# Moving TensorE operands by 64 bytes in a two-layer trunk: constants, some low parts, and seven 16-column products

## The chip, the cores and the metric

The kernel runs on one core of one Trainium2 chip. The metric is the device time of one execution in microseconds (us), the median of several. Below, TensorE is PE, VectorE is DVE, ScalarE is ACT, GpSimd is POOL and SyncE is SP.

## The reference

A decoder trunk of two layers over 512 tokens and 1024 channels, float32. Layer 0 mixes tokens by retention, layer 1 by an mLSTM, each with 4 heads of 256 query and key columns and 512 value columns; each layer ends in a convolutional feed-forward net (FFN) of 2816 inner columns. Cut to what matters:

```python
for i in range(2):
    mod = silu(c) @ ada_w[i] + ada_b[i]                  # 6 vectors of 1024
    h = rmsnorm(x, norm_tok_g[i]) * (1 + sc_t) + sh_t
    y = retention(h) if i == 0 else mlstm(h)             # heads: q, k, v, gate, group norm, out
    x = x + gt_t * y
    h = rmsnorm(x, norm_ffn_g[i]) * (1 + sc_f) + sh_f
    x = x + gt_f * (silu(a) * b) @ w_down                # a, b = split(conv(h @ w_up))
return rmsnorm(x, final_g)
```

## The kernel before, in words

**Precision.** Matrix products run in TensorE's fp32r form on operands that are split in a high and a low part. A product of two split matrices is three TensorE products: high by high, high by low, low by high. In names, `whi` and `wlo` are the parts of a weight tile, `hh` and `hl` of the normalized input `h`, `yh` and `yl` of a head's output, `ggh` and `ggl` of an FFN's gated columns, and so on. A weight tile has 128 partitions and 1024 columns of 4 bytes, in a buffer of 1088 columns; most tiles begin at column 0 of their buffer, some at column 16 (`OFF`, 64 bytes later).

**Folded products.** Most projections don't use the plain block product but one of seven products for eight (`seven`, in the order 1, 2, 6, 5, 7, 4, 3). Their weights are sums and differences of weight blocks, built by DVE from two loaded tiles (`wa`, `wb` or several `wv`, through `ws` and `wt`), at column 16 of their buffers; each product is 256 columns wide. A `PairStream` has the weight blocks as TensorE's stationary operand and the tokens moving (banks `p`), a `ValueStream` the tokens stationary and the weights moving (banks `pv`). `terms(n, k)` gives the token side. DVE evacuates a product's bank by adding a copy `fs` to it (`p<-p,fs`).

**Stages.** Start and first norm to about 88 us, the heads of layer 0, the output projection with the next norm's square sums mixed in (`boundary`, near 386 us), the FFN, then the same for layer 1. `heads` sets the sequence of a layer: `q(0)`, `q(1)`, ... each with attention steps and, after `g(1)`, the first output projection `o(0)`; `contract_items` runs an output projection of one head, `boundary` the last ones, in two halves of 256 tokens, with weights at column 16. `boundary` already opens with a product of 16 columns whose result nothing reads (`short_product`), and so do the folded FFN runs (`folded`). The square sums of a norm come from `SquareSum.root`, which multiplies by a constant matrix `ones_d` of 1/1024 (bank `pms`); `ones_v` (group norm, `pmu` and `pvar`) and `ones_1` (sums, `pden`, and products that keep TensorE busy while the first loads run, `pst<-warm`) are its two relations. Between the projections DVE also computes the modulation vectors, one load `ada` of 128x1025 at a time.

**Order.** No engine's order is written by hand. All calls are recorded by a class `Plan`, so each has the line L377 in the profile, and then a planner lists them by estimated costs, due times and the number of free buffers per kind, and issues them in that order. A queue issues in order: SP, which issues most loads, waits at a load whose buffer is not free, and so do those behind it. Numbers in names of the listings below count tiles; the last is the call's position in the program.

Of the kernel before, what the change touches and what calls it, by code (L numbers as in the profile page):

```python
# [10 lines left out]
F32 = mybir.dt.float32  # L11
F32R = mybir.dt.float32r
# [4 lines left out]
P = 128  # L17
T = 512
D = 1024
KT = D // P  # L20
# [16 lines left out]
WPAD = 64  # L37
OFF = 16
# [342 lines left out]
def trunk(ctx: ExitStack, tc: tile.TileContext, xT, cb, pos, vec, ident, decay, zmask, ada, w_s0, w_in0, w_v0,  # L381
          w_o0, w_in1, w_v1, w_f1, w_o1, w_up, w_dn, out):
    nc = tc.nc
    const = ctx.enter_context(tc.tile_pool(name="const", bufs=1))
# [10 lines left out]
    def uid(s):  # L395
        count[0] += 1
        return f"{s}_{count[0]}"

    def tile_of(pool, shape, dt, tag, name):
        return Buf(pool, shape, dt, tag, name, KINDS.get(tag, 0), tag == "ps")  # L400

    def slot(s, dt=F32, w=T):
        return tile_of(slots, [P, w], dt, "s", uid(s))

    def wide(s, dt=F32):
        return tile_of(wpool, [P, WCOLS + WPAD], dt, "w", uid(s))

    def bank(s):
        return tile_of(psum, [P, T], F32, "ps", uid(s))
# [4 lines left out]
    def fixed(pool, shape, dt, name):  # L414
        b = tile_of(pool, shape, dt, name, name)
        b.get()
        return b

    plan = Plan()
    V, A, G, PE, S = (plan.engine(*p) for p in (("DVE", nc.vector), ("ACT", nc.scalar), ("POOL", nc.gpsimd),  # L420
                                                ("PE", nc.tensor), ("SP", nc.sync)))
# [3 lines left out]
    V.memset(fixed(const, [P, 32], F32, "pad")[:], 0.0)  # L425
    ones = {}
    for name, v in (("d", 1.0 / D), ("v", 1.0 / DV), ("1", 1.0)):
        o = fixed(const, [P, P], F32R, f"ones_{name}")
        V.memset(o[:].bitcast(F32), v)
        ones[name] = o  # L430


# [56 lines left out]
        return lo  # L489

    class Chunk:
        def __init__(self, src, n, off, added=False):
            self.off, self.added = off, added
            self.raw = wide("raw")[:, off : off + n]
            S.dma_start(self.raw, src)

# [1 line left out]
            self.hi = high_part(self.raw, self.off)  # L498

        def low(self):  # L500
            self.lo = (low_part_added if self.added else low_part)(self.raw, self.hi, self.off)

        def lo_at(self, at, k):
            return at * P
# [115 lines left out]
    class Pair:  # L620
# [3 lines left out]
        def split(self, src, r=slice(None), eng=None):  # L624
            A.copy(self.hi[:, r], src)
            (eng or V).tensor_tensor(self.lo[:, r], src, self.hi[:, r].bitcast(F32), op=ALU.subtract)
# [6 lines left out]
    def mm3(o, ah, al, bh, bl, start, stop):  # L633
        PE.matmul(o, ah, bh, start=start, stop=False)
        PE.matmul(o, ah, bl, start=False, stop=False)
        PE.matmul(o, al, bh, start=False, stop=stop)

    def short_product(o, w, b):


        PE.matmul(o, w, b, start=True, stop=True, skip_group_check=True)
# [64 lines left out]
    class Use:  # L706


        def __init__(self, src, n, off=0, added=False):
            self.src, self.n, self.first, self.off, self.added = src, n, None, off, added  # L710

        def make(self):
            c = Chunk(self.src, self.n, self.off, self.added)
            c.high()
            c.low()
            return c
# [16 lines left out]
    def item(uses, fn, free=True):  # L733
        for u in uses:
            if u.first is None:
                u.first = len(items)
            u.last = len(items)
        items.append((uses, fn, free))
# [1 line left out]
    bars = []  # L740
    side = []

    def proj_item(src, h, then, added=False):
        def fn(w):
            ps = bank("pp")
            for k in range(KT):
                cs = slice(k * P, k * P + P)
                mm3(ps[:], w[0].hi[:, cs], w[0].lo[:, cs], h[k].hi[:], h[k].lo[:], k == 0, k == KT - 1)
            then(ps)
        item([Use(src, KT * P, added=added)], fn)  # L750

    ORDER = (1, 2, 6, 5, 7, 4, 3)

# [42 lines left out]
                PE.matmul(o, b[0][:, ts], lo[:, cs], start=False, stop=False, skip_group_check=True)  # L796
                PE.matmul(o, b[1][:, ts], hi[:, cs], start=False, stop=sp, skip_group_check=True)

    def seven(use, streams, done, between=lambda j: None):


        fs = []

        def mk(n):
            def fn(w):
                if n == ORDER[0]:
                    for s in streams:
                        s.open(w[0])
                        fs.append(slot("fs"))
                for s, f in zip(streams, fs):  # L810
                    o = {1: s.c21, 2: s.c11, 5: s.c12, 3: s.c12}.get(n, s.c21)
                    s.product(n, o, n in s.starts)
                    if n in (1, 6, 7):
                        A.copy(f[:, HB if n == 6 else HA], s.c21)
                    if n == 7:
                        V.tensor_tensor(s.c22, s.c12, f[:, HA], op=ALU.add)
                    elif n == 2:
                        V.tensor_tensor(s.c11, s.c11, f[:, HA], op=ALU.add)
                    elif n == 3:
                        V.tensor_tensor(s.c12, s.c12, f[:, HB], op=ALU.add)  # L820
                if n == 3:
                    done(*[s.banks for s in streams])
            return fn
        for j, n in enumerate(ORDER):
            item([use], mk(n), j in FREE_STEPS)
            between(j)

    def fold_pairs(srcs, terms, thens, between=lambda j: None):

        def each(then):  # L830
            def done(bs):
                for b in bs:
                    then(b)
            return done
        for n, (src, then) in enumerate(zip(srcs, thens)):
            seven(FoldUse(src, n), [PairStream(terms, then)], each(then), lambda j: between(7 * n + j))

    def fold_values(src, terms, v, split, between=lambda j: None):

        def done(a, b):  # L840
            for ps in (a[0], b[0], a[1], b[1]):
                split(v, ps)
        seven(ValueFoldUse(src, 0), [ValueStream(terms, t) for t in range(2)], done, between)

    def folded(folds, h, terms, pairs, downs):

# [192 lines left out]
        return [piece(i) for i in range(KT // per)]  # L1039

    def contract_items(ps, between=lambda i: None):
        for i, (u, run) in enumerate(ps):
            item([u], lambda w, run=run: run(w[0], 0, T))
            between(i)
# [251 lines left out]
    def heads(st, q, v, s, g, a, mid, end, o, norm, at_last):  # L1296
# [13 lines left out]
        g(1)  # L1310
        A_(1)
        contract_items(o(0))
        mid_(1)
        q(2)
# [172 lines left out]
    def half_pair(st, name, finish):  # L1487

        got = []

        def then(ps):
            got.append(ps)
            if len(got) == 2:
                st[name] = finish(*got)
        return then

    h0 = []
    R = [dict(v=[], g=[], z=[]) for _ in range(H)]
# [10 lines left out]
    def ret_gate(i):  # L1509
        def then(ps):  # L1510
            g = slot("g")
            A.activation(g[:], ps[:], AF.Silu)
            R[i]["g"].append(g)
        return then
# [21 lines left out]
    def ret_start():  # L1536
# [4 lines left out]
        pss, ps = [bank("pst") for _ in range(5)], bank("pms")  # L1541
        pcs = [bank("pc") for _ in range(2)]
        pss += pcs
        one = ones["1"][:1, :].bitcast(F32)
        h0.extend(Pair("h") for _ in range(KT))
        wh, wl, raw, mod, sq, xrs = {}, {}, {}, {}, {}, {}

# [137 lines left out]
    sums0 = Sums(h0, {}, 0, 0)  # L1685

    def sums_early():
        sums0.make()
        sums0.turn()

    def pair_srcs(w, at):
        return [(w[at], w[at + 1]), (w[at + 2], w[at + 3])]

    def ret_q(i, between=nothing):
        thens = [half_pair(R[i], name, rope) for name in ("q", "k")]
        if i:
            fold_pairs(pair_srcs(w_in0, i * 8), sums0.terms, thens, between)
            return
        for n, then in enumerate(thens):
            for j in range(2):  # L1700
                proj_item(w_in0[i * 8 + 2 * n + j], h0, then)
        item([], lambda w: sums_early())

    def ret_g(i):
        fold_pairs(pair_srcs(w_in0, i * 8 + 4), sums0.terms, [ret_gate(i)] * 2)

    def ret_v(i, between=nothing):
        fold_values(w_v0[i - 1], sums0.terms, R[i]["v"], center_split, between)

    def load_x():  # L1710
        for m in range(KT):
# [14 lines left out]
    M = [dict(v=[], o=[], z=[], q=[], k=[]) for _ in range(H)]  # L1726
# [72 lines left out]
    def ml_gate(i):  # L1799
        def then(ps):  # L1800
            o = slot("o")
            A.activation(o[:], ps[:], AF.Sigmoid)
            M[i]["o"].append(o)
        return then
# [30 lines left out]

    def ml_q(i, between=nothing):
        thens = [lambda ps, name=name, n=iter((0, 1)): conv_then(i, name, next(n))(ps) for name in ("q", "k")]
        fold_pairs(pair_srcs(w_in1, 1 + i * 8), start1.sums.terms, thens, between)

    def ml_g(i):  # L1840
        fold_pairs(pair_srcs(w_in1, 5 + i * 8), start1.sums.terms, [ml_gate(i)] * 2)

    def ml_o(i):
        return pieces(lambda j: w_o1[i, j], 4, gate_col(1, 0), lambda k: M[i]["y"][k], i in O_ADDED)

    def ml_v(i, between=nothing):
        fold_values(w_f1[i - 1], start1.sums.terms, M[i]["v"], plain_split, between)

    start1 = Start([w_in1[j] for j in (0, 5, 6, 7)], h1, 1, 0, [gates, ml_gate(0), ml_gate(0), ml_gate(0)], True)
    ffn0.items(start1)  # L1850
# [152 lines left out]
```

## Time and profile before

| | before |
|---|---|
| median of 3 runs | 1513.67 us (1513.44 to 1513.98) |
| the profiled execution | 1513.25 us, of which the span is 1511.3 us |
| mean granted TensorE clock | 0.994 |
| busy share PE / PEld / DVE / ACT / POOL | 98% / 91% / 84% / 71% / 19% |
| HBM read | 195.23 MB, 131 GB/s over the span |
| the longest wait of PE | 5.5 us, for DVE, before 291.87 us |

All times of the profile count from the span's start. In a timeline a row has the start, the busy time of one or several instructions of a form, the engine, the line, the operation, what it writes from what it reads, and its shape; the idle time before it stands in brackets, with what ended it. A matmul's busy time overlaps with that of its successor, so a start-to-start distance says more of a stream of matmuls than their durations. In the windows a row has its length, then for each engine asked for its busy time and count, then the granted clock, the DMA share and GB/s.

### The profile page before, as it was taken

Reading aid. Unit: us, or ns where it says so; the run is one execution under the profiler, and the core shown is the slowest. Engines: PE = TensorE matmul, PEld = TensorE weight load, DVE = VectorE, ACT = ScalarE, POOL = GpSimd, SP = SyncE. Lnnn points to the kernel's source line nnn. Section 1 sums busy time; section 2 is a strip of 40 time slices with the busy share of each in tenths; the row PEclk is TensorE's granted clock in tenths of the full one; section 3 lists DMA queues with packets and bytes.
Section 4 is the critical chain, followed back from the end, with each engine's and each line's share of the span. In section 5 each row is a group of like instructions: output and inputs, shape, how many; then the busy total and the mean of one; then the engine's idle time right before and its main releaser. Section 6 shows DMA issues by size and latency. Waiting matters only on the chain.

```text
span 1511.3 us, 27097 instructions
## 1 busy us (share of the span) xinstructions
PE 1477.9 (98%) x10405; PEld 1375.5 (91%) x10405; DVE 1262.9 (84%) x2123; ACT 1069.0 (71%) x1593; POOL 281.6 (19%) x311
## 2 busy tenths in 40 slices
PE   9999999899999999999999999999999999999997
PEld 6889999798998989899998988999989899999997
DVE  6998989676887888888798999999877877877786
ACT  4558858777577666666578986899976867677662
POOL 0234222232111111111001222223131111111100
PEclk9999999999999999999999999999999999999999
DMA  9467999896487999999368887989875868787841
GB/s 375 158 161 204 282 272 275 207 236 148 103 224 202 244 265 255 271 260 253 115 168 223 206 234 202 262 216 248 223 179 136 213 171 196 173 207 182 204 127 56
DMA packets 92979, 314.98 MB, mean 208 GB/s; under 512 B 12193, under 2 KB 14625, under 8 KB 92850
## 3 DMA queue, kind: packets, MB, share of 16 engines
q0 software_dynamic: 31824, 115.88, 41.4%
q1 hardware_dynamic: 61026, 197.38, 36.7%
q8 instruction: 81, 1.33, 0.3%
q14 instruction: 48, 0.39, 0.1%
HBM read 195.23 MB, written 2.12 MB: 131 GB/s over the span
## 4 chain that ended last, share of the span: by engine, by line
PE 85%; DVE 6%; DMA 6%; ACT 2%; issue 1%; POOL 0%; SPq 0%; DVEq 0%; ACTq 0%; POOLq 0%
PE p L377 31%; PE po L377 25%; PE pv L377 9%; PE pp L377 6%; PE pf L377 4%; PE pav L377 4%; PE pst L377 3%; PE psc L377 2%; DMA wb<-w_up 1%; DMA ada<-ada 1%; PE pc L377 1%; ACT whi L377 1%; DVE ws L377 1%; DVE wlo L377 1%; DVE ada L377 1%
## 5 line engine op out<-in xcount | busy, mean ns | idle before, releaser
L377 PE MATMUL p<-hh,whi 128*128 128x256 f32 (+1 forms) x962 | 267.8, 279 | 5.8 <-DVE p L377 5.5
L377 PE MATMUL p<-hl,whi 128*128 128x256 f32 x960 | 266.8, 278 | 0.7 <-DVE hl L377 0.5
L377 PE MATMUL p<-hh,wlo 128*128 128x256 f32 x960 | 265.3, 278 | 1.5 <-DMA wlo<-wa 1.5
L377 ACT ACTIVATE wlo<-whi 128x1024 fp32r<-128x1024 f32 x221 | 233.2, 1059 | 45.5 <-PE po L377 22.0
L377 PEld LDWEIGHTS p<-hh,whi 128*128 128x128 f32 x962 | 181.5, 189 | 7.7 <-DVE p L377 6.0
L377 PEld LDWEIGHTS p<-hl,whi 128*128 128x128 f32 x960 | 181.3, 189 | 1.5 <-DVE hl L377 1.1
L377 PEld LDWEIGHTS p<-hh,wlo 128*128 128x128 f32 x960 | 180.3, 189 | 2.0 <-DMA wlo<-wa 1.9
L377 PE MATMUL p<-t24h,whi 128*128 128x256 f32 x720 | 161.3, 281 | 6.9 <-DVE p L377 4.2
L377 DVE SCALAR_TENSOR_TENSOR x<-po,mod,x 128x512 f32<-128x512 f32 (+1 forms) x184 | 113.6, 629 | 52.5 <-PE po L377 51.7
L377 PE MATMUL po<-ggh,wlo 128*128 128x512 f32 (+1 forms) x448 | 152.6, 343 | 0.8 <-DVE wlo L377 0.8
L377 PE MATMUL po<-ggl,whi 128*128 128x512 f32 (+1 forms) x448 | 153.1, 343 | 0.0
L377 PE MATMUL po<-ggh,whi 128*128 128x512 f32 (+1 forms) x448 | 152.6, 343 | 0.0
L377 ACT CAST whi<-raw 128x1024 fp32r<-128x1024 f32 (+1 forms) x121 | 121.8, 1019 | 26.0 <-PE po L377 7.8
L377 PE MATMUL p<-t24l,whi 128*128 128x256 f32 x480 | 133.6, 278 | 0.0
L377 PEld LDWEIGHTS p<-t24h,whi 128*128 128x128 f32 x720 | 123.0, 189 | 10.8 <-DVE p L377 5.9
L377 DVE SCALAR_TENSOR_TENSOR ada<-ada,c_ext 128x1025 f32<-128x1025 f32 x96 | 122.0, 1275 | 10.4 <-DMA ada<-ada 10.4
L377 POOL DMA_DIRECT2D wlo<-wa x60 | 53.0, 883 | 414.7 <-ACT wlo L377 320.1
L377 PE MATMUL po<-yh,whi 128*128 128x256 f32 (+1 forms) x354 | 116.0, 329 | 0.0
L377 PE MATMUL po<-yl,whi 128*128 128x256 f32 (+1 forms) x352 | 115.7, 329 | 0.0
L377 PE MATMUL po<-yh,wlo 128*128 128x256 f32 (+1 forms) x352 | 115.7, 329 | 0.0
L377 ACT CAST whi<-ws 128x1024 fp32r<-128x1024 f32 x84 | 88.0, 1050 | 30.9 <-DVE ws L377 22.3
L377 DVE TENSOR_TENSOR wlo<-raw,whi 128x768 fp32r<-128x768 f32 (+2 forms) x113 | 101.8, 915 | 7.7 <-ACT whi L377 3.6
(285 smaller groups left out, 4459.8 us busy)
## 6 DMA issues: line engine op xcount, KB each, us to landing
ada<-ada SPq DMA_DIRECT2D x96, 512.5 KB, 6.9
wlo<-ws POOLq DMA_DIRECT2D x71, 512.0 KB, 7.1
wlo<-wa POOLq DMA_DIRECT2D x60, 512.0 KB, 6.7
wlo<-wt POOLq DMA_DIRECT2D x44, 512.0 KB, 7.7
wlo<-raw POOLq DMA_DIRECT2D x40, 512.0 KB, 8.4
wa<-w_up SPq DMA_DIRECT2D x34, 512.0 KB, 5.8
wb<-w_up SPq DMA_DIRECT2D x34, 512.0 KB, 6.8
raw<-w_o SPq DMA_DIRECT2D x32, 512.0 KB, 7.2
```

Source lines behind the costliest of these rows:

```text
L377: getattr(c.obj, c.name)(*[real(v) for v in c.a], **{key: real(v) for key, v in c.k.items()})
```

## The change

Three things change. The constant matrices `ones_d`, `ones_v` and `ones_1` become 192 columns wide and are used from column 16 on, so their data begins 64 bytes later than before. `Chunk`, `Use` and `proj_item` get an argument `lo_off`: the low part of the last tile of each `contract_items` call, and that of the last key tile of layer 0's first head, begin at column 16 instead of 0. And `seven` gets an argument `lead`: seven of the folded calls open with a product of 16 columns, with `ones_1` as weights, into a part of a bank that nothing reads before it is written again. These are layer 0's `v` of head 1, `g` of head 2 and `q` of head 3, and layer 1's `q` of heads 1 and 3, `v` of head 1 and `g` of head 2. The constants' pool grows by 768 bytes a partition, so every other tile keeps its place modulo 128 bytes. The arithmetic is the same.

```diff
-        o = fixed(const, [P, P], F32R, f"ones_{name}")
-        V.memset(o[:].bitcast(F32), v)
+        o = fixed(const, [P, P + WPAD], F32R, f"ones_{name}")[:, OFF : OFF + P]
+        V.memset(o.bitcast(F32), v)
...
     class Chunk:
-        def __init__(self, src, n, off, added=False):
-            self.off, self.added = off, added
+        def __init__(self, src, n, off, added=False, lo_off=0):
+            self.off, self.added, self.lo_off = off, added, max(off, lo_off)
...
-            self.lo = (low_part_added if self.added else low_part)(self.raw, self.hi, self.off)
+            self.lo = (low_part_added if self.added else low_part)(self.raw, self.hi, self.lo_off)
...
-    def seven(use, streams, done, between=lambda j: None):
+    def seven(use, streams, done, between=lambda j: None, lead=False):
...
+                    if lead:
+                        short_product(streams[0].c22[:, :16], ones["1"], streams[0].terms(1, 0)[0][:, :16])
...
     def contract_items(ps, between=lambda i: None):
+        ps[-1][0].lo_off = OFF
...
-                proj_item(w_in0[i * 8 + 2 * n + j], h0, then)
+                proj_item(w_in0[i * 8 + 2 * n + j], h0, then, lo_off=OFF * n * j)
...
-            fold_pairs(pair_srcs(w_in0, i * 8), sums0.terms, thens, between)
+            fold_pairs(pair_srcs(w_in0, i * 8), sums0.terms, thens, between, i == 3)
...
-        fold_pairs(pair_srcs(w_in0, i * 8 + 4), sums0.terms, [ret_gate(i)] * 2)
+        fold_pairs(pair_srcs(w_in0, i * 8 + 4), sums0.terms, [ret_gate(i)] * 2, lead=i == 2)
...
-        fold_values(w_v0[i - 1], sums0.terms, R[i]["v"], center_split, between)
+        fold_values(w_v0[i - 1], sums0.terms, R[i]["v"], center_split, between, i == 1)
...
-        fold_pairs(pair_srcs(w_in1, 1 + i * 8), start1.sums.terms, thens, between)
+        fold_pairs(pair_srcs(w_in1, 1 + i * 8), start1.sums.terms, thens, between, i in (1, 3))
...
```

TensorE, layer 0, where the projection `q` of head 3 begins its second bank pair (`p2_589` is a half of it, `pav` the attention of head 2). Before:

```order
1621 L377 MATMUL pav_567_3102<-sh_522_3030,vh_509_2985 128x256
1622 L377 MATMUL pav_567_3102<-sl_523_3052,vh_509_2985 128x256
1623 L377 MATMUL pav_567_3102<-sh_522_3030,vl_510_3063 128x256
1624 L377 MATMUL p2_589_3124<-hh_24_237,whi_579_2853 128x256
1625 L377 MATMUL p2_589_3124<-hl_25_265,whi_579_2853 128x256
```

Of the changed kernel:

```order
1624 L377 MATMUL pav_567_3080<-sl_523_3092,vh_509_2987 128x256
1625 L377 MATMUL pav_567_3080<-sh_522_3032,vl_510_3090 128x256
1626 L377 MATMUL p2_589_3131<-hh_24_237,ones_1_81 128x16
1627 L377 MATMUL p2_589_3131<-hh_24_237,whi_579_2852 128x256
1628 L377 MATMUL p2_589_3131<-hl_25_265,whi_579_2852 128x256
```

The 16-column product stands directly ahead of the folded run, as it does in the six other places. The planner also lists three stretches of the heads otherwise than before, about 126 to 340, 830 to 895 and 1068 to 1100 us; the FFNs and the norms keep their order.

DVE, layer 0, before PE's longest wait. `ada_540` and `ada_539` are loads of the modulation, each step frees its buffer; `ws`, `wt` and `wlo` build folded weights; `wa_600` and `wb_601` are loaded tiles. Before:

```order
356 L377 SCALAR_TENSOR_TENSOR vl_506_3040<-vt_503_2822,vm_504_2823,vh_505_2979 128x512
357 L377 TENSOR_TENSOR sl_523_3052<-sp_521_2994,sh_522_3030 128x256
...
366 L377 TENSOR_TENSOR wt_605_3112<-wa_600_2826,ws_604_3087 128x512
367 L377 SCALAR_TENSOR_TENSOR ada_539_2814,mod_0_86<-ada_539_2814,c_ext_82 128x1025
368 L377 SCALAR_TENSOR_TENSOR ada_540_2981,mod_0_86<-ada_540_2981,c_ext_82 128x1025
369 L377 TENSOR_TENSOR p1_588_3142<-p1_588_3142,fs_590_3154 128x256
```

Of the changed kernel:

```order
356 L377 TENSOR_TENSOR wt_582_3041<-wa_577_2756,ws_581_2995 128x512
357 L377 TENSOR_TENSOR p1_536_2768<-p1_536_2768,fs_538_2772 128x256
358 L377 SCALAR_TENSOR_TENSOR ada_540_2983,mod_0_86<-ada_540_2983,c_ext_82 128x1025
359 L377 SCALAR_TENSOR_TENSOR vl_506_3077<-vt_503_2783,vm_504_2784,vh_505_2981 128x512
...
368 L377 TENSOR_TENSOR wt_605_3135<-wa_600_2830,ws_604_3101 128x512
369 L377 SCALAR_TENSOR_TENSOR ada_539_2801,mod_0_86<-ada_539_2801,c_ext_82 128x1025
370 L377 TENSOR_TENSOR p1_588_3152<-p1_588_3152,fs_590_3157 128x256
```

The step of `ada_540` moved from row 368 to row 358, ahead of ten rows that build weights and attention operands.

SP's queue at the same place (`tab` is a table of decays). Before:

```order
102 L377 DMA tab_511_2785<-decay 128x512
103 L377 DMA ada_539_2814<-ada 128x1025
104 L377 DMA wa_600_2826<-w_in0 128x1024
105 L377 DMA wb_601_2891<-w_in0 128x1024
106 L377 DMA ada_540_2981<-ada 128x1025
107 L377 DMA wv_624_3080<-w_v0 128x1024
108 L377 DMA ada_557_3149<-ada 128x1025
109 L377 DMA wv_622_3159<-w_v0 128x1024
```

Of the changed kernel:

```order
102 L377 DMA ada_539_2801<-ada 128x1025
103 L377 DMA tab_511_2809<-decay 128x512
104 L377 DMA wa_600_2830<-w_in0 128x1024
105 L377 DMA wb_601_2920<-w_in0 128x1024
106 L377 DMA ada_540_2983<-ada 128x1025
107 L377 DMA wv_624_3063<-w_v0 128x1024
108 L377 DMA ada_557_3082<-ada 128x1025
109 L377 DMA wv_622_3169<-w_v0 128x1024
```

Here only `tab` and `ada_539` have changed places. `ada_557` takes the buffer of `ada_539` in the order before and that of `ada_540` in the changed one, and `wv_622` stands behind it in both.

More of the change, by code (lines that the diff above doesn't have):

```diff
@@ L706, in trunk, with __init__ @@
     class Use:
-        def __init__(self, src, n, off=0, added=False):
-            self.src, self.n, self.first, self.off, self.added = src, n, None, off, added
+        def __init__(self, src, n, off=0, added=False, lo_off=0):
+            self.src, self.n, self.first, self.off, self.added, self.lo_off = src, n, None, off, added, lo_off
         def make(self):
-            c = Chunk(self.src, self.n, self.off, self.added)
+            c = Chunk(self.src, self.n, self.off, self.added, self.lo_off)
             c.high()
@@ L741, in trunk, with proj_item @@
     side = []
-    def proj_item(src, h, then, added=False):
+    def proj_item(src, h, then, added=False, lo_off=0):
         def fn(w):
@@ L749, in fn @@
             then(ps)
-        item([Use(src, KT * P, added=added)], fn)
+        item([Use(src, KT * P, added=added, lo_off=lo_off)], fn)
     ORDER = (1, 2, 6, 5, 7, 4, 3)
@@ L826, in seven, with fold_pairs @@
             between(j)
-    def fold_pairs(srcs, terms, thens, between=lambda j: None):
+    def fold_pairs(srcs, terms, thens, between=lambda j: None, lead=False):
         def each(then):
@@ L835, in fold_pairs, with fold_values @@
         for n, (src, then) in enumerate(zip(srcs, thens)):
-            seven(FoldUse(src, n), [PairStream(terms, then)], each(then), lambda j: between(7 * n + j))
-    def fold_values(src, terms, v, split, between=lambda j: None):
+            seven(FoldUse(src, n), [PairStream(terms, then)], each(then), lambda j: between(7 * n + j), lead and not n)
+    def fold_values(src, terms, v, split, between=lambda j: None, lead=False):
         def done(a, b):
@@ L842, in done @@
                 split(v, ps)
-        seven(ValueFoldUse(src, 0), [ValueStream(terms, t) for t in range(2)], done, between)
+        seven(ValueFoldUse(src, 0), [ValueStream(terms, t) for t in range(2)], done, between, lead)
     def folded(folds, h, terms, pairs, downs):
@@ L1543, in ret_start @@
         pss += pcs
-        one = ones["1"][:1, :].bitcast(F32)
+        one = ones["1"][:1].bitcast(F32)
         h0.extend(Pair("h") for _ in range(KT))
@@ L1837, in ml_q @@
         thens = [lambda ps, name=name, n=iter((0, 1)): conv_then(i, name, next(n))(ps) for name in ("q", "k")]
-        fold_pairs(pair_srcs(w_in1, 1 + i * 8), start1.sums.terms, thens, between)
+        fold_pairs(pair_srcs(w_in1, 1 + i * 8), start1.sums.terms, thens, between, i in (1, 3))
     def ml_g(i):
-        fold_pairs(pair_srcs(w_in1, 5 + i * 8), start1.sums.terms, [ml_gate(i)] * 2)
+        fold_pairs(pair_srcs(w_in1, 5 + i * 8), start1.sums.terms, [ml_gate(i)] * 2, lead=i == 2)
     def ml_o(i):
@@ L1846, in ml_v @@
     def ml_v(i, between=nothing):
-        fold_values(w_f1[i - 1], start1.sums.terms, M[i]["v"], plain_split, between)
+        fold_values(w_f1[i - 1], start1.sums.terms, M[i]["v"], plain_split, between, i == 1)
     start1 = Start([w_in1[j] for j in (0, 5, 6, 7)], h1, 1, 0, [gates, ml_gate(0), ml_gate(0), ml_gate(0)], True)
```

## The prediction, before the run

> **What bounds the kernel now.** I read the page's busy shares first, then the chain, then the list of waits.
>
> ```profile
> PE 1477.9 (98%) x10405; PEld 1375.5 (91%) x10405; DVE 1262.9 (84%) x2123; ACT 1069.0 (71%) x1593; POOL 281.6 (19%) x311
> PE 85%; DVE 6%; DMA 6%; ACT 2%; issue 1%; POOL 0%; SPq 0%; DVEq 0%; ACTq 0%; POOLq 0%
> PE p L377 <- DVE p L377: 9.7, 6, 5.5
> PE pv L377 <- DVE wlo L377: 0.8, 1, 0.8
> ```
>
> TensorE (PE) is busy 98% of the span and owns 85% of the last chain. There are two ways to a shorter time: the same products closer together, or shorter waits. The whole profiled execution took 1513.25 us, 1.95 more than its span of 1511.3, and lies 0.42 under the median of 1513.67. I sum against 1513.25 and add 0.42 at the end. 0.2% is 3.03 us, about what a measurement of this kernel can tell from no change.
>
> How close together are the products? The timeline of PE around the first normalization's square sums:
>
> ```profile
> 405.04 0.28 PE L377 MATMUL po<-yh,whi 128*128 128x256 f32 x1
> ...
> 405.72 0.28 PE L377 MATMUL pms<-ssh,ones_d 128*128 128x256 f32 x1
> ...
> 406.19 0.28 PE L377 MATMUL po<-yh,wlo 128*128 128x256 f32 x1
> ```
>
> From 405.04 to 405.72 six steps from start to start take 0.68 us, 113 ns each. The row at 405.72 is the first of a pair with `ones_d` as weights (tile `pms`, the squares' mean). From it to 406.19 four steps take 0.47 us, 118 ns each, in the same loop with the same shapes. The windows show that each pace lasts:
>
> ```profile
> 387.00:405.70 18.70, 18.70 (x167) 1.00 0.34 105
> 405.70:442.90 37.20, 37.20 (x318) 1.00 0.72 170
> 751.30:767.30 16.00, 15.97 (x134) 1.00 0.67 180
> 1146.20:1183.40 37.20, 37.20 (x318) 1.00 0.71 170
> 1487.00:1499.70 12.70, 12.70 (x110) 1.00 0.00 1
> ```
>
> A window counts the two products that are still running at its start, so it holds two starts fewer than its count: 18.70/165 = 113.3 ns before the pair, 37.20/316 = 117.7 after it, 12.70/108 = 117.6 at the end. The granted clock is 1.00 in all five. I call them the fast and the slow pace; one slow product costs 4.4 ns. What separates the pair is where its operands lie in their partitions. By the tile sizes in the code, the boundary's weights begin 64 bytes past a multiple of 128 and the moving tiles at a multiple; in the `pms` pair both begin at a multiple. That an even pair sets the slow pace, and that it then stays until something else resets it, is my reading of these rows. Two more fit it. A run that follows 512-column products with both operands even is slow; a run that follows one with odd weights (the low part of an FFN's last output tile) is fast:
>
> ```profile
> 198.55 0.28 PE L377 MATMUL p<-hh,whi 128*128 128x256 f32 x1
> ...
> 199.14 0.28 PE L377 MATMUL p<-hh,wlo 128*128 128x256 f32 x1
> ...
> 483.47 0.39 PE L377 MATMUL po<-ggl,whi 128*128 128x512 f32 x1
> 483.69 0.40 PE L377 MATMUL po<-ggh,wlo 128*128 128x512 f32 x1
> 483.93 0.28 PE L377 MATMUL p<-t3h,whi 128*128 128x256 f32 x1
> ...
> 484.39 0.28 PE L377 MATMUL p<-t3l,whi 128*128 128x256 f32 x1
> ```
>
> Five steps from 198.55 take 0.59 us, 118 ns each; four steps from 483.93 take 0.46 us, 115 ns each, the first of them still slow.
>
> **The change part by part. Constants.** With `ones_d` odd, the `pms` products get the boundary's own arrangement (odd weights, even moving), so nothing sets the slow pace at 405.72. Gain: 316 x 4.4 ns = 1.39 us at the first boundary, 1.39 at the third, 108 x 4.4 = 0.48 at the last. At the second (751 to 767) it is 132 x 4.4 = 0.58, but PE meets the wait of 0.8 us for DVE's `wlo` soon after, so I count 0.3. Sum 3.55. All of it is PE time on the chain, with no other engine late: in these windows PE is busy to the last hundredth. Bounds: 0, if the pair sets the pace for another reason than its address, and 3.84.
>
> **Low parts of the output tiles.** Each of six `contract_items` calls now has 8 products of 512 columns with odd weights. The row at 483.69 shows one: 0.24 us to the next start, where the one before takes 0.22. I take 16 ns each, 48 x 16 = 0.77 us; bounds 5 and 25 ns (0.24 and 1.2 us). The two calls of `o(0)` lie in the heads ahead of waits, so 32 x 16 ns = 0.51 counts. The 16 key products of the first head (0.26 us by the same price) lie ahead of DVE's waits and count nothing.
>
> **Leads.** Seven 16-column products, priced at the one that opens a boundary:
>
> ```profile
> 386.55 0.40 PE L377 MATMUL po<-yh,whi 128*128 128x16 f32 x2
> ...
> 387.02 0.28 PE L377 MATMUL po<-yh,whi 128*128 128x256 f32 x1
> ```
>
> From 386.55 to 387.02 stand one short product and three long ones (the first is counted in its row, x2): 0.47 - 3 x 0.113 = 0.13 us for the short one, 0.9 us for seven. Each may buy the fast pace for its call: 168 products x 4.4 ns = 0.74 us at most, 5.2 for seven, less what is fast already. But the heads are not bound by PE alone:
>
> ```profile
> 836.00:1083.00 247.00, 242.16 (x1851) 231.59 (x1850) 232.72 (x364) 211.60 (x322) 64.27 (x72) 1.00 0.89 230
> 200.00:260.00 60.00, 59.92 (x493) 58.75 (x492) 54.85 (x85) 44.77 (x71) 17.22 (x20) 1.00 1.03 277
> 260.00:270.00 10.00, 10.00 (x75) 9.64 (x74) 9.79 (x20) 8.73 (x12) 1.89 (x4) 1.00 0.60 171
> 290.00:300.00 10.00, 7.41 (x41) 7.12 (x42) 6.62 (x13) 4.39 (x6) 2.19 (x2) 0.66 0.79 182
> ```
>
> In the second layer's heads (836 to 1083) DVE, the third busy figure, works 232.72 of 247 us; in the first's (200 to 260) the DMA share is 1.03. A PE that comes sooner waits sooner. I count 0 for gains less leads, bounds -2.5 and +0.9. The other uses of the constants (the warm-up products at the start, `pmu`, `pvar`, `pden`) I put at 0.2 us together, an estimate by the same 16 ns for about a dozen that nothing covers. Without the order, then: -3.55 + 0.51 + 0.2 = **-2.8 us**.
>
> **The order.** The leads cost the planner TensorE time, and three stretches come out in another order (about 126 to 340, 830 to 895 and 1068 to 1100 us); the feed-forward nets keep theirs. The place where that can weigh is PE's longest wait:
>
> ```profile
> 291.87 0.58 PE L377 MATMUL p<-hh,whi 128*128 128x256 f32 x1 [5.47 <-DVE p L377]
> 258.55 0.33 SPq L377 DMA_DIRECT2D ada<-ada  x1
> 264.23 0.63 DVE L377 TENSOR_TENSOR sl<-sp,sh 128x256 fp32r<-128x256 f32 x2
> 270.38 1.23 DVE L377 SCALAR_TENSOR_TENSOR ada<-ada,c_ext 128x1025 f32<-128x1025 f32 x1
> 271.64 0.33 SPq L377 DMA_DIRECT2D ada<-ada  x1
> 272.07 1.63 SPq L377 DMA_DIRECT2D wv<-w_v  x2
> 287.51 2.82 DVE L377 SCALAR_TENSOR_TENSOR ada<-ada,c_ext 128x1025 f32<-128x1025 f32 x1 [3.55 <-DMA ada<-ada]
> 291.39 0.42 DVE L377 TENSOR_TENSOR p<-p,fs 128x256 f32<-128x256 f32 x1
> ```
>
> Read backwards: PE at 291.87 waits for the evacuation of a bank at 291.39, which stands on DVE behind the `ada` step at 287.51, which waited 3.55 us for its load; that load is behind two others that SP could issue only at 271.64, since an `ada` load stood in front until DVE's `ada` step of 270.38 freed its buffer. Meanwhile the DMA share fell to 0.60 (260 to 270). In the changed order DVE does `ada_540`'s step ten rows sooner, before the `sl` steps that began at 264.23, and the blocked load takes its buffer: free at about 264.8 + 1.2 = 266.0 (an estimate; two `wt` steps and an evacuation come before it) instead of 271.6, so that load goes into the idle stretch. The two `wv` loads behind it still need a buffer that DVE's `wt` reads about 271: only one load of 512 KB is out of their way, about 2 us at 277 GB/s. So the wait shrinks by about **2 us**. Bounds: the wait goes wholly, or grows by 4.
>
> A wait that shrinks below some length saves more:
>
> ```profile
> 295.24 0.41 PE L377 MATMUL p<-t3h,wlo 128*128 128x256 f32 x1
> 295.45 0.41 PE L377 MATMUL p<-t3h,whi 128*128 128x256 f32 x1
> ```
>
> After it the products start 0.21 us apart, at the granted clock of 0.66 that the window 290 to 300 shows, until about 296.7: (296.7 - 291.9)/0.21 = 23 products, each 0.1 us dearer, 2.2 us. The Trainium skill, page "TensorE: Matmul & The Clock Gate", Part 1, says the clock drops to half after an idle window of about 3.4 us; by it a wait cut to 3.4 us would save these 2.2 too. The row agrees for 5.47 us; no wait of 3 to 5 us is shown here. I count nothing for it.
>
> Forecast: 1513.25 - 2.8 - 2.0 = 1508.4, and 0.42 for the median: about **1508.8 us**.
>
> **The rivals.** (a) Only the boundaries gain, and the heads give back what the order saves: -2.8, so 1510.9, at the edge of what can be told. For it speaks DVE's 94% in the second layer's heads; against it the unused DMA stretch.
>
> (b) The long wait goes wholly, and with it the half clock: -2.8 - 5.5 - 2.2 + 0.9 (the leads then count) = -9.6, so 1504.1. Against it: the `wv` loads' buffer.
>
> (c) Slower: `ada_540`'s step now stands sooner in DVE's queue than its load lands. That load was issued at 258.55; DVE reaches the step about 264.8. If it lands at 268.3, DVE stands 3.5 us with `ws`, `wt` and `wlo` of two folded tiles behind it, and the `wv` loads that need their buffers go out as much later. The wait at 286 then grows by 3.5, and a second wait of like size, with a half clock of its own, opens where the delayed `wlo` lands, about 275: -2.8 + 3.5 + 3.5 + 2.2 = +6.4, so 1520.1; half of that delay gives 1515 to 1517. It decides from about 2 us of delay. For it: the DMA share of 1.03 before 260. Against: its share of 0.60 from 260 to 270 says that the earlier loads had run out by about 266.
>
> (d) Addresses have no part in the pace, and the pair flips it for another reason (the change of weights, say). Then the change only pays its leads: 1513.67 + 0.9 = 1514.6. The Trainium skill, "SBUF — State Buffer", Who interferes with whom, gives TensorE two independent read ports and says that it waits on nobody; by that page there is nothing to gain from an address. The two paces at clock 1.00 speak against that page's rule, though not for the address by themselves.
>
> **How the numbers follow.** Chances: forecast 0.40, (a) 0.22, (b) 0.10, (c) 0.18, (d) 0.10. Faster by over 0.2% is below 1510.64: nearly all of the forecast (0.38), half of (a) less a little (0.10) and (b): 0.58. Slower by over 0.2% is above 1516.70: most of (c) (0.15) and a tail of (d) (0.03): 0.18. The rest, 0.24, is the same. The range reaches from (b)'s 1504 to 1517, which leaves out half of (b) and about half of (c), 0.05 + 0.09; the forecast's own range is 1506 to 1511.
>
> **What would show it.** Right: starts 113 ns apart through 406 to 443, 1146 to 1183 and 1487 to 1500 us (some 316 starts in 35.8 us instead of 37.2); 113 ns after the last output tile of `o(0)` and after each lead; the wait before the bank that comes after 286 at 3 to 4 us; the blocked `ada` load issued near 266. Wrong: 118 ns after an odd `pms` pair (then (d)); the wait at 286 as long or longer, or a new one near 275 (then (c)); the heads' stretch 836 to 1083 longer than 247 us.

## The result: slower by 0.56%

The changed kernel took 1523.56 us in the median of 6 runs against 1513.95 us before; the ratio is 1.0056 with a 95% interval of 1.0042 to 1.0070, that is 8.5 us more (6.4 to 10.6). One of the six runs, 1835.16 us at a granted clock of 0.753, is not in the ratio. The profiled execution took 1520.49 us, its span is 1518.7.

The page of the changed kernel, and its list of waits of PE:

```profile
PE 1480.1 (97%) x10412; PEld 1376.2 (91%) x10412; DVE 1261.3 (83%) x2123; ACT 1068.6 (70%) x1593; POOL 282.2 (19%) x311
PE 80%; DMA 8%; DVE 5%; issue 3%; ACT 2%; POOL 0%; SPq 0%; DVEq 0%; POOLq 0%; ACTq 0%
PE p L377 <- DVE p L377: 8.7, 8, 2.7
PE p L377 <- DMA wlo<-wa: 1.7, 1, 1.7
PE pv L377 <- DMA wlo<-wv: 1.4, 1, 1.4
```

The longest wait of PE for DVE fell from 5.5 to 2.7 us, in the direction of the forecast, but there are more waits (eight for an evacuation instead of six, and one of 1.4 us for `wlo<-wv`), and PE owns 80% of the last chain instead of 85%. Where the time went is read by following the same product through both traces, start in the changed kernel minus start before:

| product at, before (us) | 122 | 171 | 329 | 374 | 404 | 480 | 541 | 647 | 828 | 903 | 1030 | 1054 | 1085 | 1130 | 1176 | 1501 |
|---|---|---|---|---|---|---|---|---|---|---|---|---|---|---|---|---|
| later by (us) | 0.0 | 1.2 | -1.5 | -1.3 | -0.5 | -0.3 | -1.7 | -0.1 | 0.3 | 2.0 | 3.0 | 4.5 | 6.9 | 7.3 | 7.9 | 7.4 |

Layer 0's heads win 1.5 us, both output boundaries lose 0.6 to 0.8 instead of winning (374 to 404, 1130 to 1176), and layer 1's heads lose 6.6 (828 to 1085). The steps of 1.5 us in layer 0's FFN (480 to 647) cancel; instructions and order are the same there.

The windows over the first boundary (before its square sums, then after them), the second boundary, the last norm, and the heads of layer 1:

```profile
385.64:404.34 18.70, 18.70 (x160) 1.00 0.32 99
404.34:442.30 37.96, 37.96 (x324) 1.00 0.70 167
750.00:766.50 16.50, 15.78 (x140) 1.00 0.67 183
1494.60:1507.30 12.70, 12.70 (x115) 1.00 0.00 0
837.00:1091.00 254.00, 244.24 (x1859) 233.10 (x1858) 235.23 (x364) 213.56 (x324) 64.97 (x72) 1.00 0.87 224
```

The first boundary runs at 18.70/158 = 118 ns from its first product on, where before it opened at 113 and fell to 118 at `pms`. Having opened slow, it gains nothing from the moved `ones_d` behind `pms` (37.96/322 = 118 ns). Where the stretch ahead of `pms` is fast, it now stays fast: in the last norm it is 12.70/113 = 112 ns, against 118 before. The heads of layer 1 take 254 us instead of 247; PE stands still in 254.0 - 244.24 = 9.8 of them instead of 247.0 - 242.16 = 4.8, so 5 of the 7 us are more waiting.

How the boundary now opens, in the timeline of PE:

```profile
384.95 0.39 PE L377 MATMUL po<-yl,whi 128*128 128x512 f32 x1
385.18 0.40 PE L377 MATMUL po<-yh,wlo 128*128 128x512 f32 x1
385.41 0.39 PE L377 MATMUL po<-yh,whi 128*128 128x16 f32 x2
385.64 0.28 PE L377 MATMUL po<-yl,whi 128*128 128x256 f32 x1
...
386.35 0.28 PE L377 MATMUL po<-yl,whi 128*128 128x256 f32 x1
```

The opening product of 16 columns is the same as before. What is new is that a product with odd weights stands ahead of it (`yh,wlo`, a moved low part; odd means that the data begin 64 bytes past a multiple of 128 bytes, even that they begin at one). Then six steps from 385.64 take 0.71 us, 118 ns each.

### The profile page after: what moved, and what is told of

Same layout as the page of the kernel before. It is cut to its first block, busy times and chain, and to the rows that moved or that the text cites. A ratio compares the mean times of both kernels' runs of the same rounds, so it can differ in the third digit from the quotient of the medians.

```text
span 1518.7 us, 27130 instructions
## 1 busy us (share of the span) xinstructions
PE 1480.1 (97%) x10412; PEld 1376.2 (91%) x10412; DVE 1261.3 (83%) x2123; ACT 1068.6 (70%) x1593; POOL 282.2 (19%) x311
## 4 chain that ended last, share of the span: by engine, by line
PE 80%; DMA 8%; DVE 5%; issue 3%; ACT 2%; POOL 0%; SPq 0%; DVEq 0%; POOLq 0%; ACTq 0%
PE p L377 29%; PE po L377 24%; PE pv L377 7%; PE pp L377 6%; PE pf L377 4%; PE pav L377 4%; PE pst L377 3%; DMA wlo<-ws 2%; PE psc L377 2%; PE pc L377 1%; ACT whi L377 1%; DMA ada<-ada 1%; DMA wb<-w_up 1%; DMA wlo<-wa 1%; DVE ws L377 1%
```

## The experiments

**First group: the parts by themselves.** `ones_only` moves the three constants and nothing else. Its core:

```diff
-        o = fixed(const, [P, P], F32R, f"ones_{name}")
+        o = fixed(const, [P, P + WPAD], F32R, f"ones_{name}")[:, OFF : OFF + P]
```

> Before, with the constants moved by 64 bytes and nothing else; the order of every engine is that of before. If the address of the pms weights sets the pace, products after pms stay 113 ns apart at all four boundaries: 3.5 us less than before, about 1510.4. If the pair flips the pace for another reason than its address: no change, 1514.

Measured: 0.9986 (0.9973 to 0.9999), 2.1 us less. The windows of the third boundary, before and after `pms`, and the last norm:

```profile
1130.80:1149.40 18.60, 18.60 (x167) 1.00 0.36 113
1149.40:1185.60 36.20, 36.20 (x321) 1.00 0.73 175
1490.00:1502.00 12.00, 12.00 (x108) 1.00 0.00 0
```

36.20/319 = 113 ns behind `pms` now. The address sets the pace there, and this part of the prediction is shown. The interval of the time, 0.2 to 4.1 us less, holds the 3.5 of the sum. In this trace, though, not all four boundaries are fast. In the first, a step of 0.37 us from start to start at 419 us (0.11 is usual) is followed by the slow pace for the rest of the run; `mended`, below, waits for a low part at the same product. The second is slow from 726 us on, before `pms`. Windows ahead of its `pms`, in the kernel before and then in `ones_only`:

```profile
732.00:751.00 19.00, 19.00 (x170) 1.00 0.22 66
733.00:752.00 19.00, 19.00 (x164) 1.00 0.23 61
```

19.00/168 = 113 ns against 19.00/162 = 117. Products, order and places modulo 128 bytes are the same in this stretch. In both traces one step where it begins is long, 0.131 us in the kernel before (at 725.67) and 0.135 in `ones_only` (at 726.05); the first settles on the fast pace behind it, the second on the slow one. `order_l0`, below, where even the addresses are those of before, also has 0.135 there and is slow behind it. So a pace can also turn without a difference in these. What `pms` does to it has no exception in the traces, by the starts of the products there: in the eight kernels with even `ones_d`, the products behind `pms` go at 118 ns at all four boundaries; in the five with odd `ones_d` they keep the pace that they had ahead of it, 15 times the fast and 5 times the slow one.

`all_old_order` has the whole change in the order of before. The planner doesn't see the leads; each is issued with the first product of its run:

```diff
-                        short_product(streams[0].c22[:, :16], ones["1"], streams[0].terms(1, 0)[0][:, :16])
+                        c0 = streams[0].c11 if isinstance(streams[0], ValueStream) else streams[0].c22
+                        plan.ahead = (c0[:, :16], ones["1"], streams[0].terms(1, 0)[0][:, :16])
```

> The whole change, but in the order of before: the seven 16-column products are issued right ahead of the first product of their run, without being listed by the planner. Theory O (the new order of the heads costs the time): close to before, 1512 to 1515, and PE's waits as before. Theory P (the pace after the leads and the odd low parts costs the time): 1519 to 1523, like the change.

Measured: 1.0020 (1.0009 to 1.0032), 3.0 us more: between the two theories, a part of the loss.

`new_order_only` is the other half: the leads are recorded and ordered, and then skipped when the calls are issued; nothing is moved by 64 bytes.

```diff
+                        plan.calls[-1].skip = True
...
+            if c.skip:
+                continue
```

> The changed kernel's order on every engine, but the seven 16-column products are not issued, and constants and low parts lie as before. Theory O: 1519 to 1523, nearly all of the loss, with the waits of the changed kernel in the second layer's heads. Theory P: 1512 to 1514, since the long wait near 286 us shrinks by 2 us and nothing else changes.

Measured: 1.0036 (1.0023 to 1.0048), 5.5 us more. The two halves add up to the change: 0.36% + 0.20% = 0.56%. So the order costs about two thirds of the loss, and the moved addresses with the leads one third. No run has the leads with odd weights alone, so their own share of that third is not measured.

`pace` measures the pace alone.

> TensorE alone, nothing of the reference is computed: 40 stretches of 24 products of a context (512 columns both even; 256 both even; 512 with every third weight odd; 256 odd weights at the fast pace), then an opener (none; 16 columns odd weights; 16 even; two of 16 odd; 16 with an odd moving side), then 24 products of 256 columns with odd weights, or with an odd moving side. If a 16-column product sets the fast pace by itself, all stretches behind an odd one run at 113 ns. If it depends on what stands ahead of it, as the changed kernel's trace suggests, then 113 ns only behind even 512-column products, and 118 ns behind even 256-column products, behind odd 512-column ones and behind a run at the fast pace.

Mean start-to-start distance of the last products in each stretch, in ns, worked out from the trace of its one execution (w: odd weights and even moving side, as in `p`; m: the reverse, as in `pv`):

| what stands ahead | no opener | 16 odd weights | 16 even | two of 16 odd | 16 odd moving |
|---|---|---|---|---|---|
| 512 columns, even | w 118, m 118 | w **113**, m 118 | w 118, m **113** | w 118, m 118 | w 118, m **113** |
| 256 columns, even | w 118, m 118 | w 118, m 118 | w **113**, m 118 | w **113**, m 118 | w 118, m 118 |
| 512, every third odd | w **113**, m 118 | w 118, m 118 | w 118, m 118 | w **113**, m **113** | w 118, m 118 |
| 256 odd, at 113 | w **113**, m **113** | w 118, m **113** | w 118, m 118 | w **113**, m 118 | w 118, m 118 |

Two stretches of its timeline, both behind 256 even columns and ahead of odd weights: first the opener with odd weights, then with even ones.

```profile
112.08 0.39 PE L398 MATMUL b<-mh,hi 128*128 128x16 f32 x2
112.31 0.28 PE L398 MATMUL b<-ml,hi 128*128 128x256 f32 x1
...
112.78 0.28 PE L398 MATMUL b<-mh,lo 128*128 128x256 f32 x1
...
123.72 0.39 PE L398 MATMUL b<-mh,hi 128*128 128x16 f32 x2
...
124.42 0.28 PE L398 MATMUL b<-mh,lo 128*128 128x256 f32 x1
...
124.76 0.28 PE L398 MATMUL b<-mh,lo 128*128 128x256 f32 x1
```

From 112.31 four steps take 0.47 us and stay at 118; from 124.42 three take 0.34, 113 each. An opener doesn't set a pace by itself: what follows depends on what stands ahead of it as well, and a second opener undoes the first in three of the four `w` cases. Behind even 512-column products the odd opener gives 113, as at the boundaries before. Behind 512-column products of which every third has odd weights, the change's own, the same opener gives 118. For five of the change's seven leads the table gives 118: four stand behind 256 even columns, one ahead of a `w` run and behind a run at 113. For `w` runs the odd opener came out as expected in all four rows; an `m` run behind one at 113 stayed fast. The 512-column products of the third row take 231.1 ns on average, once they are steady, against 226.7 for even ones: 24 of them are longer by (231.1 - 226.7) x 24 us/1000 = 0.1 us, or 13 ns per odd product.

**Second group: which order, and which address.** In `order_l0` and `order_l1` the planner lists the leads of one layer only, and none is issued, in the manner of `new_order_only`; for layer 1, for instance, one of the lines taken back from the changed kernel is:

```diff
-        fold_values(w_v0[i - 1], sums0.terms, R[i]["v"], center_split, between, i == 1)
+        fold_values(w_v0[i - 1], sums0.terms, R[i]["v"], center_split, between)
```

> The order alone, in part: the planner lists the leads of layer 0 only, none is issued, addresses as before. If layer 0's new order is the gain that was forecast (the long wait near 286 us shorter) and layer 1's the loss: 1 to 2 us less than before. If the loss lies in layer 0: 4 to 6 us more.

> The order alone, the other part: the planner lists the leads of layer 1 only, none is issued, addresses as before. If layer 1's new order is the loss: 6 to 8 us more than before, with new waits of PE between 1045 and 1085 us of the span. If the loss lies in layer 0: as before within 1 us.

Measured: layer 0 alone 0.9992 (0.9977 to 1.0007), 1.2 us less but within the spread; layer 1 alone 1.0047 (1.0034 to 1.0059), 7.1 us more. The loss by order is layer 1's.

`lows_only` keeps the moved low parts and drops the constants' edit and the leads; its core is:

```diff
     def contract_items(ps, between=lambda i: None):
+        ps[-1][0].lo_off = OFF
```

> Before with the low parts moved (last tile of each output projection call, and the key tile), in the order of before, constants even, no leads. If an odd 512-column product ahead of the boundary's opening product sets the slow pace: both output boundaries start at 118 ns, 2 x 165 x 4.4 ns = 1.5 us more; 48 odd products cost 13 ns each, 0.6 us; the runs after o(0) go fast, up to 0.9 us less where nothing else waits. Together 1 to 2 us more than before. If low parts only cost what they take: 0.6 us more, boundaries fast.

Measured: 1.0024 (1.0015 to 1.0033), 3.6 us more. The window of the first boundary's first half:

```profile
389.34:408.04 18.70, 18.70 (x160) 1.00 0.32 101
```

18.70/158 = 118 ns, where 113 stood before; the third boundary is the same. That is 1.5 us, and the odd products' own 48 x 13 ns are 0.6. The gain of up to 0.9 us behind `o(0)` did not last: the runs from 200 us on do go at 113, but near 236 PE meets a wait of 1.1 us for a copy `fs` that the trace of before does not have. The rest of the 3.6 is not told apart; the interval's lower end (2.3) is near the sum of the first two.

`leads_even` has four leads with even weights in the order of before, where the table gives 113. Against `all_old_order`, which has the leads odd:

```diff
-                        plan.ahead = (c0[:, :16], ones["1"], streams[0].terms(1, 0)[0][:, :16])
+                        plan.ahead = (c0[:, :16], ones["1"][:], streams[0].terms(1, 0)[0][:, :16])
```

> Before with four leads (g of head 2 and q of head 3 in layer 0, v of head 1 and g of head 2 in layer 1) whose weights stay even, issued in the order of before. From the stretches measured by themselves: an even 16-column product behind even 256-column ones (or, for v, behind even 512-column ones) sets 113 ns. So these runs should start at 113 ns where odd leads gave 118. If the heads are bound by PE: 1 to 2 us less than before. If DVE and transfers bind them: within 0.7 us of before, the time given back as waits.

Measured: 0.9998 (0.9987 to 1.0010). The timeline of PE, behind the lead of `g` of head 2 in layer 0 in this kernel:

```profile
244.65 0.28 PE L384 MATMUL p<-hh,whi 128*128 128x256 f32 x1
...
245.11 0.28 PE L384 MATMUL p<-hl,whi 128*128 128x256 f32 x1
```

and in the changed kernel:

```profile
245.22 0.28 PE L377 MATMUL p<-hh,whi 128*128 128x256 f32 x1
...
245.70 0.28 PE L377 MATMUL p<-hl,whi 128*128 128x256 f32 x1
```

0.46 us for four steps that settle at 113, against 0.48 at 118 throughout. Three of the four runs went fast, and the time did not move: in the heads a faster PE gains nothing that can be told from zero. For `v` the pace stayed at 118, against the table; two `pden` products stand directly ahead of it, behind 256-column ones, a context that `pace` does not have.

**Third group: one lead each, and two versions that should be better.** `order_mq3` lists `q` of head 3 alone, `order_mv1` `v` of head 1 alone, both of layer 1, neither issued.

> The order alone: the planner lists one lead, that of q of head 3 in layer 1, which is not issued; addresses as before. From the traces, the rows it moves lie at 1045 to 1085 us, where the layer-1 order lost 4 us: expected 3.5 to 5 us more than before, with PE's waits for DVE near 1073 and for a low part near 1081 us. If the loss needs the other leads too: within 1 us of before.

> The order alone: the planner lists one lead, that of v of head 1 in layer 1, which is not issued; addresses as before. The rows it moves lie at 830 to 895 us, where the layer-1 order lost 2.5 to 3 us: expected 2 to 3 us more than before, and no loss at 1045 to 1085.

Measured: 1.0025 (1.0013 to 1.0037), 3.8 us, and 1.0018 (1.0006 to 1.0030), 2.7 us. Together 0.43%, which within the intervals answers for layer 1's 0.47%. Behind the lead of `q` the waits of PE between 1030 and 1100 us are, before first and then in `order_mq3`:

```profile
PE p L377 <- DVE p L377: 0.7, 1, 0.7
PE pv L377 <- DVE z L377: 0.2, 1, 0.2
```

```profile
PE p L380 <- DVE p L380: 1.6, 2, 1.0
PE p L380 <- DMA wlo<-ws: 1.0, 1, 1.0
PE pv L380 <- DVE wlo L380: 0.8, 1, 0.8
PE pv L380 <- DVE z L380: 0.2, 1, 0.2
```

That is 3.6 us of waits instead of 0.9. The changed kernel has them too; its timelines of DVE and PE show what makes them:

```profile
1070.68 0.69 DVE L377 TENSOR_TENSOR whi<-wb,whi 128x512 fp32r<-128x512 f32 x1 [0.98 <-ACT whi L377]
1071.64 1.53 DVE L377 SCALAR_TENSOR_TENSOR mc<-p,vecs,mc 128x511 f32<-128x511 f32 x2 [0.26 <-ACT mc L377]
1073.16 0.69 DVE L377 TENSOR_TENSOR whi<-wb,whi 128x512 fp32r<-128x512 f32 x1
1073.77 0.43 DVE L377 TENSOR_TENSOR p<-p,fs 128x256 f32<-128x256 f32 x1
```

```profile
1074.25 0.39 PE L377 MATMUL p<-t24h,whi 128*128 128x256 f32 x1 [1.01 <-DVE p L377]
1081.87 0.39 PE L377 MATMUL p<-t24h,wlo 128*128 128x256 f32 x1 [1.01 <-DMA wlo<-ws]
```

The evacuation at 1073.77, for which PE waits, now stands on DVE behind two `whi` steps and two `mc` steps, and two of these waited for ACT first. Some seven microseconds later a low part arrives late. DVE was not short of time in sum (235 us of 254): by these rows its queue was in the wrong order for PE.

`ones_order_l0` takes the two edits that had looked good; it makes only `ones_d` odd and lists layer 0's leads without issuing them:

```diff
+        off = OFF * (name == "d")
+        o = fixed(const, [P, P + WPAD], F32R, f"ones_{name}")[:, off : off + P]
```

> ones_d moved by 64 bytes (the other constants even), and layer 0 in its new order (its leads listed, not issued). If both small gains add: 3 to 4 us less than before, 0.2 to 0.25%. If layer 0's order gives nothing: 2 us less, as the constants alone.

Measured: 0.9995 (0.9976 to 1.0015). `mended` corrects the change by the table, in the order of before: `ones_d` odd as above, even leads in three runs, and

```diff
+        if at_o0:
+            ps[-1][0].lo_off = OFF
```

> In the order of before: ones_d moved by 64 bytes, odd low parts only in the calls for o(0), leads with even weights for g of head 2 and q of head 3 in layer 0 and g of head 2 in layer 1. By the measured stretches all of these runs and all boundaries are fast. If the pace in the heads counts: 4 us or more less than before. If only the boundaries count: 2 us less, as the constants alone.

Measured: 0.9992 (0.9981 to 1.0004). Neither can be told from before, nor from `ones_only`, whose 0.9986 is the lowest ratio of all. In `mended`'s trace the boundaries open fast and pass `pms` fast. Two windows of its first boundary, and a row of PE between them:

```profile
387.50:420.70 33.20, 33.20 (x294) 1.00 0.46 118
421.60:443.40 21.80, 21.80 (x187) 1.00 0.76 192
```

```profile
421.35 0.39 PE L384 MATMUL pf<-hh,wlo 128*128 128x256 f32 x1 [0.25 <-DMA wlo<-raw]
```

33.20/292 = 114 ns until PE, now faster, meets a short wait for a low part; behind it 21.80/185 = 118. Part of what the pace wins is given back so, in the boundary as in the heads.

## Why the prediction was wrong

**The paces, and what an odd `pms` pair does: right.** `ones_only` shows the address at work, by 2.1 us (0.2 to 4.1) against the 3.5 of the sum. Rival (d), that addresses have no part, falls: behind `pms` the same products go from 118 to 113 ns at clock 1.00 when only the constants' address differs. The Trainium skill's "SBUF — State Buffer", Who interferes with whom, says that TensorE never waits on anyone; from that (d) had concluded that there is nothing to gain from an address, and the measurement decides against the conclusion.

**The low parts of the output tiles: wrong in kind.** The prediction priced each odd product at 16 ns (13 measured) and took the boundaries' fast opening as given. It counted on the opening product of a boundary and quoted a fast run behind odd 512-column products, and never asked what the one does after the other. Together they give the slow pace. So the gains counted at the first and third boundary, 2 x 1.39 us, were not there, and 2 x 0.74 was lost ahead of `pms`.

**The leads: no fast pace, and little lost by it.** "Each may buy the fast pace": in the changed kernel six of the seven runs go at 118 ns, and only `v` of head 1 in layer 1 at 113. `q` of head 3 in layer 1 even lost the fast pace that it had before (nine steps from 1020.10 us take 1.02 us before, seven from 1023.07 take 0.82 in the changed kernel). The changed kernel's order puts attention products (`psc`, `pav`), even on both sides, directly ahead of three leads in layer 0 and one in layer 1; what an opener does behind such products was not asked. That the heads hide a faster pace was right (`leads_even`, 0.9998).

**The order: the step that failed most.** I costed the one stretch where before has a long wait, layer 0, with a gain of 2 us, and its mechanism did not come about. The changed kernel's rows:

```profile
268.51 0.33 SPq L377 DMA_DIRECT2D ada<-ada  x1
274.90 0.33 SPq L377 DMA_DIRECT2D wv<-w_v  x1
284.31 1.23 DVE L377 TENSOR_TENSOR ws<-wv,wv 128x1024 f32<-128x1024 f32 x1 [4.97 <-DMA wv<-w_v]
285.45 0.43 DVE L377 TENSOR_TENSOR p<-p,fs 128x256 f32<-128x256 f32 x1
285.93 0.38 PE L377 MATMUL p<-t24h,whi 128*128 128x256 f32 x1 [2.72 <-DVE p L377]
291.23 0.43 DVE L377 TENSOR_TENSOR p<-p,fs 128x256 f32<-128x256 f32 x1 [1.09 <-ACT whi L377]
292.32 0.28 PE L377 MATMUL p<-hh,whi 128*128 128x256 f32 x1
```

The blocked `ada` load went out earlier, at 268.5 instead of 271.6, but the `wv` loads did not, at 274.9 instead of 272.1. Counting like instructions from the start, the evacuation of 291.39 stands here at 291.23, and the product that waited for it starts at 292.32 instead of 291.87: the wait's end came no sooner. The new order had made PE 3.2 us later by 270, and the shorter wait only wins that back. PE now stands still earlier and shorter, 2.72 us for an evacuation that has come to stand behind `ws`, and ahead of 292 it does products that before were done ahead of the long wait. What was won came after it. At 292.32 the changed kernel is 0.45 us later than before, at 297 it is 1.2 us earlier, and the clock is what differs in between. Windows of the half clock, before and then of the changed kernel:

```profile
290.70:297.50 6.80, 5.27 (x23) 0.50 0.70 132
287.30:290.70 3.40, 3.40 (x18) 0.50 1.08 231
```

That is the term that the prediction named and counted as nothing. All in all layer 0's order gave 1.2 us, not distinguishable from nothing. For the two stretches of layer 1 the sum had no term at all, since before shows no long wait there. They cost 7.1 us. Rival (c) had the right kind of mechanism, work that comes to stand ahead of an evacuation, in the wrong layer, and it was the only slower case by order that got a chance; that its 1520 lies near the measured time is luck.

## What to carry to other kernels

Where a planner sets the order, even seven instructions that it reckons at 0.06 us each re-deal the queues of other engines, and a stretch without waits has only waits to win: give every reordered stretch a price, above all those that run well. Try the address or the instruction in the old order first, so that the two effects come apart. When a pace depends on what went before, read each new neighbour pair from the order, and measure all combinations in one small run before any is built in.

## What the runs showed of the hardware

A stream of 256-column products with one operand odd and the other even has two paces at a granted clock of 1.00, 113.3 and 117.8 ns; with both even it took 120 ns in `pace`. Which of the two it takes depends on whether weights and moving side begin at a multiple of 128 bytes or 64 bytes past one, and on what ran before. The table has this for the contexts of `pace`; `v` in `leads_even` and the second boundary in `ones_only` show that it is not all. The pace then stays, in the boundaries for over 300 products, until a pause or a product of another kind ends it; of the `pms` pairs only the even ones do. Why an opener turns it was not tried.

The clock fell to 0.50 after waits of PE well under 3.4 us: after 2.72 us in the changed kernel (from 287.3 us on, above), and after 1.75 us in `order_mv1`. A wait of 3.22 us in `order_l1` left it at 1.00. The row that ends the wait and the window behind it, first of `order_mv1`, then of `order_l1`:

```profile
823.43 0.38 PE L380 MATMUL p<-t24h,whi 128*128 128x256 f32 x1 [1.75 <-DVE p L380]
823.90:827.30 3.40, 3.40 (x19) 0.50 1.06 262
905.22 0.38 PE L380 MATMUL p<-hh,wlo 128*128 128x256 f32 x1 [3.22 <-DMA wlo<-wa]
905.20:908.60 3.40, 2.90 (x23) 1.00 1.05 213
```

So the length of a single wait does not decide it by itself. The prediction had weighed a rule of about 3.4 us (the Trainium skill, "TensorE: Matmul & The Clock Gate", Part 1); shorter waits were followed by the half clock too.

The kernel before varied more in the experiments than at first, 1509.14 to 1522.02 us in one group of 35 runs, so effects under about 2 us stayed open.
